# Attention probabilities transposed by VectorE and a trip through DRAM instead of by TensorE

## The chip, the core and the metric

The kernel runs on one core of one Trainium2 chip. The metric is the device time of one execution in microseconds, as the median of several executions. One profiled execution gives the trace; its own time stands beside its span below.

## The reference, cut to what matters

One decoder layer over a prompt of 1024 tokens and 32 sample tokens (8 sequences of 4), all in float32, with a model width of 1024. The input is normed and projected (`h @ w_in`) into thirteen parts. Two branches follow: four mLSTM heads (`mq`, `mk`, `mv` with gates) and sliding-window attention with sinks (`aq`, `ak`, `av`; eight query heads over two key/value heads, window 128). Both are gated, projected by `w_m_out` and `w_a_out`, gated again (`ga`, `gm`), summed and projected by `w_out`; a residual and a final norm end it. The change touches the attention of the prompt:

```
s = jnp.einsum('bnqkgd,bnskd->bnkgqs', qg, k.astype(f32)) * (A_HEAD_DIM ** -0.5)
s = jnp.where(mask[None, :, None, None], s, -jnp.inf)
mx = jnp.maximum(jnp.max(s, axis=-1, keepdims=True), sink)
p = jnp.exp(s - mx)
den = jnp.sum(p, axis=-1, keepdims=True) + jnp.exp(sink - mx)
o = jnp.einsum('bnkgqs,bnskd->bnqkgd', p / den, v.astype(f32))
```

Each block of 128 queries sees its own 128 keys and the 128 before them. In the last product the keys are summed over, so the probabilities are wanted with keys on the partitions, while the softmax makes them with queries on the partitions. This turn is what the change does in another way.

## The kernel before

**The stream.** TensorE works through one long list of projections in a fixed order. A job (`job`, `piece`) is one block of 128 output columns against all tokens, in three pieces of 384, 384 and 288 tokens, with each float32 operand split into a high and a low part (`wh`, `wl`, `h_h`, `h_l`) and three products for each of the eight blocks of the model width. The order is `ak`, `av`, `aq` 0 to 3, then `mq`, `mk`, `mv` of heads 0 and 1, `mq`, `mk` of head 2. Then come pairs of jobs multiplied together with fewer products (`block_products`, results `bx`, `bw`, `by`, `bz`), whose operands `t1` to `t4` are sums of blocks of `h` that the generator `sum_blocks` forms; it starts when job `mq` of head 1 starts. Last come the two output projections and `w_out`.

**Work at the side.** Everything else of TensorE's (attention, mLSTM heads, samples, the gates' ada chunk) is written as generators. The planner `Side` keeps a clock `side.now` that each matmul of the stream advances by its estimated length; `side.tick` after each group of three products lets generators take a step when their time has come and the PSUM bank that they ask for is free. A generator yields the lag until its next step and the banks. Each stream of generators has a limit of live ones and a gap between starts: `"m": (2, 35.0)` for the mLSTM heads, `"a": (5,8.0)` for the attention. So the order of TensorE's instructions is set while the program is written out, and it is kept (`in_order`). The other engines' orders follow from it, with loads that can go earlier moved up by the tile scheduler.

**A unit of attention.** `unit(g, b0)` does two blocks of queries for the pair of heads (g, g+4): 16 units in all. It loads queries, keys and values (`uqv`, `ukv`), 12 us later makes scores (`sc`, eight or fewer matmuls), masks and takes maxima on VectorE (`p`, `mx`, `nmx`), exponentials on ScalarE, the reciprocal of the sum on VectorE, and scales `p` (kv head 0 on VectorE, 1 on ScalarE). Then TensorE transposes `p` into the bank `pt` (`tr` with the identity in `cst`, 8 transposes of 128x128, 6 where `b0` is 0), ScalarE and VectorE copy `pt` back over `p`, and 16 (or 12) matmuls make `oT`. ScalarE copies `oT` to SBUF and the result goes to DRAM (`oD`).

**Loads and stores.** All loads and nearly all stores are issued by SyncE's queue (SP) in order: `dma` at once, `store` with a delay of 4.0 of the planner's clock, so that SP doesn't wait for a result that is not there yet. A load of a tensor first issues its own due stores. GpSimd (POOL) issues the stores that turn a block while they write: VectorE transposes within blocks of 32x32 (`V.transpose`, STREAM_TRANSPOSE), and four DMAs then put the blocks of 32 columns in their places in DRAM in runs of 32 floats. `across` (tensors `mkN`, `mvN`) and `stage_c3` of a head (`yhD`) do that. A head's `load` reads `mkN` and `mvN` back (tiles `hkn`, `hv`) with four other loads, and its next step is planned 9 or 10 us later.

**Buffers.** Most SBUF tiles come from one ring of 43 (`ht`); PSUM has two banks for each of `g`, `a`, `b`, `o`. In the trace nearly every instruction of VectorE, ScalarE and GpSimd has line L219 (the wrapper that records the order), matmuls L258, transposes on TensorE L263, DMAs of SP L246.

Of the kernel before, what the change touches and what calls it, by code (L numbers as in the profile page):

```python
# [23 lines left out]
NT = 4  # L24
# [87 lines left out]
class Side:  # L112
# [4 lines left out]
    def __init__(self, each, limits, quiet):  # L117
        self.each, self.free = each, {}
        self.now, self.last, self.quiet, self.products = 0.0, 0.0, quiet, 0
        self.streams = {n: {"max": m, "gap": g, "wait": [], "live": [], "next": 0.0} for n, (m, g) in limits.items()}  # L120
# [52 lines left out]
def body(tc, a):  # L173
    nc = tc.nc
    with ExitStack() as ctx:
# [55 lines left out]
        def store(out, in_):  # L231
            due.append((side.now + 4.0, out, in_))
# [11 lines left out]

        def issue(out, in_, late=False):
            ins = nc.sync.dma_start(out, in_)  # L246
            ins = getattr(ins, "ins", ins)
# [5 lines left out]
        side = Side(stores, {"m": (2, 35.0), "a": (5,8.0), "x": (2, 0.0), "s": (1, 0.0), "g": (1, 0.0)}, 1.5)  # L253
# [553 lines left out]
        def unit(g, b0):  # L807
# [3 lines left out]
            qv, kv_ = ht([128, 4, 128], "uqv"), ht([128, 4, 128], "ukv")  # L811
            q, kT = qv[:, 0:2].rearrange("p c e -> p (c e)"), kv_[:, 0:3].rearrange("p c e -> p (c e)")
            vn = kv_[:, 3], qv[:, 2], qv[:, 3]
# [51 lines left out]
            for j in range(n0, 4):  # L865
                i, hf = divmod(j, 2)
                for kv in range(2):
                    r = slice(64 * kv, 64 * kv + 64)
                    mm(oT[r, i], vn[i + hf][:, r], pT[kv][:, j], start=(hf == 0 or b0 + i == 0), stop=(hf == 1))
            c0 = b0 * 128  # L870
            o = qv[:, 0:2].rearrange("p c e -> p (c e)")
            S.copy(o, oT.rearrange("p c e -> p (c e)"))
            store(oD[g][:, c0:c0 + 256], o)
# [106 lines left out]
        def head_jobs(h):  # L980
            def keep(n, smp, scale):
                def ev(p, acc, c0, w):
# [8 lines left out]
                    store(mD[h][n == "mk"][:, c0:c0 + m], t[:, :m])  # L991
# [29 lines left out]
        def across(h, n, src, c0):  # L1021
            m = src.shape[1]
            t = ht([128, 512], f"{n}t")[:, :m]
            V.transpose(t, src)
            for b in range(0, 128, 32):
                nc.gpsimd.dma_start(mN[n][h][c0:c0 + m, b:b + 32].rearrange("(t p) e -> p t e", p=32), t[b:b + 32].rearrange("p (t e) -> p t e", e=32))  # L1026

        def head(h):
# [89 lines left out]
            def stage_c3(p):  # L1118
# [7 lines left out]
                for b in range(4):  # L1126
                    nc.gpsimd.dma_start(yhD[h][c0:c0 + m].rearrange("c (q i) (b e) -> b i c q e", i=32, e=32)[b], by_block(y[32 * b:32 * b + 32]))  # L1127
# [274 lines left out]
        class head_in:  # L1402
# [3 lines left out]
            def evac(self, c, th, *src):  # L1406
# [6 lines left out]
                if n == "mv":  # L1413
                    across(h, n, src[0], 512 * th)
                else:
                    if src[0] is not t or n == "mq":
                        S.activation(t, src[0], AF.Copy, scale=scale)
                    store(mD[h][n == "mk"][:, HALF[th]], t)
                    if n == "mk":
                        across(h, n, t, 512 * th)  # L1420
# [9 lines left out]
        class gate:  # L1430
# [277 lines left out]
        def ada_gate():  # L1708
            s9 = cst[:, C_S9:C_S9 + 9]
            for j in range(2):  # L1710
# [16 lines left out]
                dma(gbD[:, cj], gb[0:1])  # L1727
                for t in range(NT):
                    dma(gsD.rearrange("(b t) e -> b t e", t=NT)[:, t, cj], gb[1:9])
# [20 lines left out]

        LOADS = [(len(pairs) - 2, 7), (len(pairs) - 1, 6), (len(pairs) - 1, 7)]
# [388 lines left out]
```

## Time and profile before

| | us |
|---|---|
| median of 3 runs | 859.75 (858.84 to 860.07) |
| the profiled execution | 857.75 |
| its span, first to last instruction | 855.9 |
| TensorE (PE) busy in the span | 822.3 |
| VectorE (DVE) busy | 604.1 |
| ScalarE (ACT) busy | 390.5 |
| GpSimd (POOL) busy | 174.7 |

Busy times are unions of an engine's own instructions. PE's matmuls overlap in its pipeline, so the duration of one is longer than the time it adds; the weight loads (PEld) run beside them. The mean granted clock of TensorE is 0.992. Attention lies between 86 and 275 us of the span, the pairs between about 285 and 655 us. The time of the profiled execution is the span and 1.85 us around it, and lies 2.0 us below the median.

### The profile page before, as it was taken

What the parts mean: (1) busy time and instruction counts of PE and PEld (TensorE: products, weight loads), DVE (VectorE), ACT (ScalarE), POOL (GpSimd) and SP (SyncE); (2) the same over time, 40 slices, a digit from 0 to 9 for tenths busy, and PEclk for the clock granted to TensorE, in tenths of its full rate; (3) what the DMA queues carried; (4) which work ended last, traced back from release to release, by engine and by line L of the source; (5) the groups of instructions that cost most, each with busy time, mean ns of one, the idle gap of its engine ahead of it and who ended that gap; (6) DMA issues with size and microseconds to landing.
All of it is one profiled execution on the core that took longest, in us unless ns stands there. A gap on an engine that the chain in (4) does not pass through costs nothing. (4 is left out here: it accounts for less than half of the span.)

```text
span 855.9 us, 15332 instructions
## 1 busy us (share of the span) xinstructions
PE 822.3 (96%) x5139; PEld 686.6 (80%) x5139; DVE 604.1 (71%) x1596; ACT 390.5 (46%) x963; POOL 174.7 (20%) x236
## 2 busy tenths in 40 slices
PE   6899999999999989999999999999999999999984
PEld 3689988789789778888887777777788999967863
DVE  3787785555687778668666565978766669857987
ACT  4672356545564543555444454434443333233334
POOL 0220000330341434211111000000012032532563
PEclk9999999999999999999999999999999999999998
DMA  9995549459756765664444335553436974273322
GB/s 326 366 356 183 150 137 291 134 125 294 214 153 203 214 170 151 194 198 135 129 115 130 115 111 162 160 150 89 116 99 203 345 254 137 82 247 99 111 99 104
DMA packets 125347, 150.82 MB, mean 176 GB/s; under 512 B 29057, under 2 KB 81409, under 8 KB 125237
## 3 DMA queue, kind: packets, MB, share of 16 engines
q1 hardware_dynamic: 121044, 143.55, 53.5%
q0 software_dynamic: 4224, 6.30, 3.6%
q8 instruction: 40, 0.66, 0.3%
q14 instruction: 39, 0.31, 0.1%
HBM read 109.73 MB, written 41.08 MB: 176 GB/s over the span
## 5 line engine op out<-in xcount | busy, mean ns | idle before, releaser
L1127 POOL DMA_DIRECT2D yhD<-yt x48 | 28.9, 608 | 108.3 <-DVE yt L219 86.3
L258 PE MATMUL g_w_ao<-ya,wh_w_ao 128*128 128x384 f32 (+1 forms) x192 | 45.7, 322 | 0.1
L258 PE MATMUL g_w_mo<-ym_l,wh_w_mo 128*128 128x384 f32 (+1 forms) x192 | 45.7, 323 | 0.0
L219 ACT ACTIVATE p<-p,nmx 128x256 f32<-128x256 f32 (+1 forms) x64 | 31.0, 486 | 28.3 <-DVE nmx L219 28.3
L1026 POOL DMA_DIRECT2D mkN<-mkt x44 | 26.9, 618 | 45.5 <-DVE mkt L219 26.0
L219 DVE CUSTOM_DVE_ANT_0 p<-sc,cst,sink 128x256 f32<-128x256 f32 (+1 forms) x64 | 26.1, 463 | 11.4 <-PE sc L258 11.4
L258 PEld LDWEIGHTS g_w_ao<-ya,wh_w_ao 128*128 128x128 f32 x192 | 33.5, 188 | 0.7 <-DVE ya L219 0.6
L258 PEld LDWEIGHTS g_w_mo<-ym_l,wh_w_mo 128*128 128x128 f32 x192 | 33.5, 188 | 0.0
L258 PE MATMUL g_aq<-h_h,wh_aq 128*128 128x384 f32 (+1 forms) x96 | 32.5, 338 | 0.0
L1026 POOL DMA_DIRECT2D mvN<-mvt x40 | 24.7, 624 | 33.6 <-DVE mvt L219 12.5
L258 PE MATMUL g_aq<-h_l,wh_aq 128*128 128x384 f32 (+1 forms) x96 | 31.0, 323 | 0.0
L258 PE MATMUL g_w_mo<-ym_l,wl_w_mo 128*128 128x384 f32 (+1 forms) x96 | 31.0, 323 | 0.0
L258 PE MATMUL g_aq<-h_h,wl_aq 128*128 128x384 f32 (+1 forms) x96 | 31.0, 323 | 0.0
L258 PE MATMUL g_w_ao<-ya,wl_w_ao 128*128 128x384 f32 (+1 forms) x96 | 30.8, 321 | 0.0
L258 PE MATMUL g_mq<-h_h,wh_mq 128*128 128x384 f32 (+1 forms) x72 | 24.7, 344 | 0.8 <-ACT vs L219 0.8
L258 PE MATMUL g_mk<-h_h,wh_mk 128*128 128x384 f32 (+1 forms) x72 | 24.8, 344 | 0.0
L219 POOL TENSOR_TENSOR ya<-yr,ya 128x384 fp32r<-128x384 f32 (+1 forms) x6 | 7.3, 1222 | 80.7 <-DVE hg L219 67.4
L258 PE MATMUL g_mk<-h_l,wh_mk 128*128 128x384 f32 (+1 forms) x72 | 23.2, 323 | 0.0
L258 PE MATMUL g_mk<-h_h,wl_mk 128*128 128x384 f32 (+1 forms) x72 | 23.2, 323 | 0.0
L258 PE MATMUL g_mq<-h_h,wl_mq 128*128 128x384 f32 (+1 forms) x72 | 23.2, 322 | 0.0
L258 PE MATMUL g_mq<-h_l,wh_mq 128*128 128x384 f32 (+1 forms) x72 | 23.2, 322 | 0.0
L219 POOL COPY qs<-mk 128x32 f32<-128x32 f32 x3 | 1.4, 463 | 103.1 <-ACT mk L219 103.1
(1700 smaller groups left out, 2800.9 us busy)
## 6 DMA issues: line engine op xcount, KB each, us to landing
hb<-hD SPq DMA_DIRECT2D x24, 256.0 KB
x<-xT SPq DMA_DIRECT2D x16, 256.0 KB
early_h<-w_ada SPq DMA_DIRECT2D x8, 512.0 KB
hD<-x SPq DMA_DIRECT2D x16, 256.0 KB
adar_ga<-w_ada SPq DMA_DIRECT2D x16, 256.0 KB
wr_ga<-w SPq DMA_DIRECT2D x16, 256.0 KB
wr_gm<-w SPq DMA_DIRECT2D x16, 256.0 KB
taD<-gt SPq DMA_DIRECT2D x16, 256.0 KB
```

The source lines that it names most:

```text
L219: ins = f(*args, **kw)
L258: in_order(nc.tensor.matmul(out, lhsT, rhs, start=start, stop=stop, skip_group_check=more))
L1026: nc.gpsimd.dma_start(mN[n][h][c0:c0 + m, b:b + 32].rearrange("(t p) e -> p t e", p=32), t[b:b + 32].rearrange("p (t e) -> p t e", e=32))
L1127: nc.gpsimd.dma_start(yhD[h][c0:c0 + m].rearrange("c (q i) (b e) -> b i c q e", i=32, e=32)[b], by_block(y[32 * b:32 * b + 32]))
```

## The change

The probabilities of a unit are no longer transposed by TensorE. VectorE transposes them within 32x32 blocks into the tiles that held queries and keys (`uq`, `uk`), eight DMAs of GpSimd's queue put the blocks in place in a DRAM tensor `pD`, and two loads of SP bring them back as `pT`, at least 18.0 of the planner's clock after the stores are written out; the products follow at least 8.0 after the loads. Values are loaded with `pT` into a tile `uv` of their own, not with the queries.

Around it: eight units may live at once instead of five, with a gap of 6.5 instead of 8.0; only one mLSTM head is live until all 16 units are done (`held`); the planner counts the backlog of SP's and GpSimd's queues (`put`, `landed`); ScalarE itself issues the stores of tiles that it wrote (`oD`, the `mq` and `mk` results, the gates `taD` and `tmD`; 69 in all); other stores wait 6.0 instead of 4.0; the stores of the ada gate go through `store` instead of `dma`.

In numbers of instructions: 4195 matmuls and transposes on TensorE instead of 4315, 148 plain copies on ScalarE instead of 164, 65 transposes on VectorE instead of 33 (and 16 copies of `pt` fewer), DMA issues on SP 667 instead of 716, on ScalarE 69 instead of 0, on POOL 260 instead of 132.

```diff
         def tick(self):
             self.each()
-            for st in self.streams.values():
-                if st["wait"] and len(st["live"]) < st["max"] and self.now >= st["next"]:
+            for name, st in self.streams.items():
+                held = name in self.held and self.held[name]()
+                if st["wait"] and not held and len(st["live"]) < st["max"] and self.now >= st["next"]:
                     self.begin(st)
...
-        def store(out, in_):
-            due.append((side.now + 4.0, out, in_))
+        def store(out, in_, by=None):
+            if by is None:
+                due.append((side.now + 6.0, out, in_))
+            else:
+                by.dma_start(out, in_)
...
+        def put(eng, cost):
+            queue[eng] = max(queue[eng], side.now) + cost
+        def landed(eng, least):
+            return max(least, queue[eng] - side.now + (2.5 if eng == "sync" else 4.0))
+        def scatter(out, in_):
+            nc.gpsimd.dma_start(out, in_)
+            put("gpsimd", 0.65)
...
-        side = Side(stores, {"m": (2, 35.0), "a": (5,8.0), ...
+        side = Side(stores, {"m": (2, 35.0), "a": (8, 6.5), ...
...
-            dma(qv[:, 2:4], vnD[:, b0:b0 + 2])
-            if b0:
-                dma(vn[0], vnD[:, b0 - 1])
             yield 12.0, sc_bank[1]
...
-            yield 7.0, "b"
-            pT = [t.rearrange("p i (j e) -> p (i j) e", e=128) for t in p]
+            yield 3.0, ""
+            flat = lambda t: t.rearrange("p c e -> p (c e)")
+            for kv, t in enumerate((qv, kv_)):
+                V.transpose(flat(t)[:, n0 * 128:], flat(p[kv])[:, n0 * 128:])
+                for k in range(4):
+                    scatter(pD[kv][n0:].rearrange("c (q i) (k e) -> k i c q e", i=32, e=32)[k],
+                                        by_block(flat(t)[32 * k:32 * k + 32])[:, n0:])
+            yield landed("gpsimd", 18.0), ""
+            pT = [ht([128, 4, 128], f"pT{kv}") for kv in range(2)]
+            vn = ht([128, 4, 128], "uv")
             for kv in range(2):
-                pt = pb([128, 4, 128], f"pt{g}_{b0}_{kv}")
-                for j in range(n0, 4):
-                    tr(pt[:, j], p[kv][:, j // 2, j % 2 * 128:j % 2 * 128 + 128], ident)
-                if kv:
-                    V.tensor_copy(pT[kv][:, n0:], pt[:, n0:])
-                else:
-                    S.copy(pT[kv][:, n0:], pt[:, n0:])
-            yield 5.0, "o"
+                dma(pT[kv][:, n0:], pD[kv][n0:].rearrange("c p e -> p c e"))
+            dma(vn[:, n0:3], vnD[:, b0 - 1 + n0:b0 + 2])
+            yield landed("sync", 8.0), "o"
...
-            store(oD[g][:, c0:c0 + 256], o)
+            store(oD[g][:, c0:c0 + 256], o, nc.scalar)
...
-                    store(mD[h][n == "mk"][:, c0:c0 + m], t[:, :m])
+                    store(mD[h][n == "mk"][:, c0:c0 + m], t[:, :m], nc.scalar)
...
-                store((taD, tmD)[c][self.i][:, HALF[th]], t)
+                store((taD, tmD)[c][self.i][:, HALF[th]], t, nc.scalar)
...
-                dma(gbD[:, cj], gb[0:1])
+                store(gbD[:, cj], gb[0:1])
...
+        side.held["m"] = lambda: len(side.streams["m"]["live"]) > 0 and len(units_done) < 16
```

The next rows show TensorE's order before at the transposes of unit (1, 2), in the last piece of job `mk` of head 0. Names are output, then inputs, with the tiles' numbers; `x4` is four rows that read alike.

```order
L258 MATMUL g_mk02_2039<-h_h1_584,wl_mk0_1_1544 128x288
L263 MATMUL pt1_2_0_2056<-cst_82,p0_1820 128x128 x4
L263 MATMUL pt1_2_1_2062<-cst_82,p1_1821 128x128 x4
L258 MATMUL oT1_0_2068<-p0_1707,uqv_1476 64x128
L258 MATMUL oT1_0_2068<-p1_1708,uqv_1476 64x128
```

In the changed program the transposes are gone, and the products of unit (1, 2), which stood in job `mv` of head 0, stand in job `mq` of head 1:

```order
L276 MATMUL g_mq10_2458<-h_h0_386,wh_mq1_0_2171 128x384
L276 MATMUL g_mq10_2458<-h_l0_387,wh_mq1_0_2171 128x384
L276 MATMUL g_mq10_2458<-h_h0_386,wl_mq1_0_2172 128x384
L276 MATMUL oT1_2_2486<-pT0_2243,uv_2245 64x128
L276 MATMUL oT1_2_2486<-pT1_2244,uv_2245 64x128
```

They read `pT`, so TensorE's in-order queue now waits there for a load. POOL's queue at the same units, before only with the stores of the heads' keys (`mkN`), in the changed program:

```order
L221 COPY qs_137<-mk0_1797 128x32
L259 DMA pD1_0_0_1415<-uq_1413 32x12x32 x4
L259 DMA pD1_0_1_1416<-uk_1414 32x12x32 x4
L259 DMA mkN0_149<-mkt_1894 32x12x32 x4
L259 DMA pD1_2_0_1538<-uq_1536 32x16x32 x4
L259 DMA pD1_2_1_1539<-uk_1537 32x16x32 x4
L259 DMA mkN0_149<-mkt_2036 32x12x32 x4
```

Eight stores of a unit now stand between any two groups of four that the heads issue. SP's queue at the reloads of these units, in the changed program (`wr_` are weights of later jobs, `gsD` the stores of the ada gate):

```order
L263 DMA wr_mk2_1_3097<-w1 128x512
L263 DMA pT0_2152<-pD1_0_0_1415 128x3x128
L263 DMA wr_mv2_0_3488<-w1 128x512
L263 DMA pT1_2153<-pD1_0_1_1416 128x3x128
L263 DMA uv_2154<-vnD_115 128x256
L263 DMA uq_2231<-qD2_118 128x256
L263 DMA uk_2232<-kD_114 128x384
L263 DMA gbD_803<-gb0_1943 1x512
L263 DMA gsD_804<-gb0_1943 8x512 x4
L263 DMA pT0_2243<-pD1_2_0_1538 128x4x128
L263 DMA pT1_2244<-pD1_2_1_1539 128x4x128
```

A reload waits in this queue for GpSimd's stores to land, and the loads of weights and of later units stand behind it. On TensorE the first product of head 1 (`S1_0`), which stood in the first piece of job `mk` of head 2, now stands at the start of the pair products `bw` that read `t2`.

More of the change, by code (lines that the diff above doesn't have):

```diff
@@ L243, in dma @@
             issue(out, in_, late)
+        queue = {"sync": 0.0, "gpsimd": 0.0}
+        def put(eng, cost):
[5 more added lines that the diff above has]
+            put("gpsimd", 0.65)
         def issue(out, in_, late=False):
             ins = nc.sync.dma_start(out, in_)
+            put("sync", 0.42)
             ins = getattr(ins, "ins", ins)
@@ L251, in issue @@
             free.append(ins)
-        side = Side(stores, {"m": (2, 35.0), "a": (5,8.0), "x": (2, 0.0), "s": (1, 0.0), "g": (1, 0.0)}, 1.5)
+        side = Side(stores, {"m": (2, 35.0), "a": (8, 6.5), "x": (2, 0.0), "s": (1, 0.0), "g": (1, 0.0)}, 1.5)
         def mm(out, lhsT, rhs, start, stop, share=1, more=False):
@@ L810, in unit @@
             n0 = 1 if b0 == 0 else 0
-            qv, kv_ = ht([128, 4, 128], "uqv"), ht([128, 4, 128], "ukv")
+            qv, kv_ = ht([128, 4, 128], "uq"), ht([128, 4, 128], "uk")
             q, kT = qv[:, 0:2].rearrange("p c e -> p (c e)"), kv_[:, 0:3].rearrange("p c e -> p (c e)")
-            vn = kv_[:, 3], qv[:, 2], qv[:, 3]
+            pD = [dp.tile([4, 128, 128], F32, name=f"pD{g}_{b0}_{kv}") for kv in range(2)]
             dma(q, qD[g][:, b0 * 128:b0 * 128 + 256])
             dma(kT[:, n0 * 128:], kD[:, (b0 - 1 + n0) * 128:(b0 + 2) * 128])
-            dma(qv[:, 2:4], vnD[:, b0:b0 + 2])
-            if b0:
-                dma(vn[0], vnD[:, b0 - 1])
             yield 12.0, sc_bank[1]
@@ L1415, in evac @@
                 else:
+                    by = None
                     if src[0] is not t or n == "mq":
                         S.activation(t, src[0], AF.Copy, scale=scale)
-                    store(mD[h][n == "mk"][:, HALF[th]], t)
+                        by = nc.scalar
+                    store(mD[h][n == "mk"][:, HALF[th]], t, by)
                     if n == "mk":
@@ L1726, in ada_gate @@
                 V.tensor_scalar(gb, gb, 0.25, None, op0=ALU.mult)
-                dma(gbD[:, cj], gb[0:1])
+                store(gbD[:, cj], gb[0:1])
                 for t in range(NT):
-                    dma(gsD.rearrange("(b t) e -> b t e", t=NT)[:, t, cj], gb[1:9])
+                    store(gsD.rearrange("(b t) e -> b t e", t=NT)[:, t, cj], gb[1:9])
                 yield 3.0, "b" if j == 0 else ""
```

9 lines of the change are left out of this document (5 added, 4 removed).

## The prediction

> **What bounds the kernel now.** I read the busy times first, then the same by stage, then what TensorE waits for. The first two lines are the page's busy times; then, for three stretches, their start and end, length, busy time of each engine with instructions, granted clock, DMA share and GB/s.
>
> ```profile
> PE 822.3 (96%) x5139; PEld 686.6 (80%) x5139; DVE 604.1 (71%) x1596; ACT 390.5 (46%) x963; POOL 174.7 (20%) x236
> ...
> 0.00:95.00 95.00, 85.01 (x572) 66.64 (x574) 64.74 (x188) 47.65 (x87) 11.62 (x25) 1.00 0.84 293
> 95.00:285.00 190.00, 187.66 (x1434) 164.54 (x1435) 127.01 (x450) 100.52 (x316) 42.44 (x72) 1.00 0.66 189
> 345.00:660.00 315.00, 314.12 (x1846) 250.51 (x1845) 222.15 (x563) 148.42 (x340) 26.28 (x51) 1.00 0.47 138
> ```
>
> TensorE is the bound: in the attention's stretch it works 187.7 of 190 us, and in the pairs after it 314.1 of 315, at full clock. So work that leaves TensorE between 95 and 285 us brings the end forward by as much, as long as no other engine or transfer then makes it wait; behind 345 us there is no slack that could swallow it. What TensorE waits for between 95 and 345 us (total, times, longest):
>
> ```profile
> PE bx L258 <- DVE f3r_w L219: 2.3, 1, 2.3
> PE pt L263 <- ACT p L219: 1.5, 2, 0.8
> PE bw L258 <- DVE t2l L219: 1.2, 1, 1.2
> PE g_mq L258 <- ACT vs L219: 0.8, 1, 0.8
> ```
>
> No load is among them: heads and units bring their operands through DRAM already, and are planned early enough.
>
> **Step 1, removed: 120 transposes on TensorE.** Groups by form (count, busy us, mean ns), then one unit in order of time:
>
> ```profile
> L263 PE MATMUL pt<-cst,p 128*128 128x128 f32 x120 | 16.3, 275 | 1.5 <-ACT p L219 1.5
> L263 PEld LDWEIGHTS pt<-cst,p 128*128 128x128 f32 x120 | 13.8, 140 | 2.8 <-ACT p L219 2.0 <-issue 0.5
> ...
> 259.59 1.09 PE L263 MATMUL pt<-cst,p 128*128 128x128 f32 x8
> 260.44 0.42 PE L258 MATMUL g_mq<-h_h,wh_mq 128*128 128x384 f32 x1
> 260.70 0.34 PE L258 MATMUL g_mq<-h_l,wh_mq 128*128 128x384 f32 x1
> 260.87 0.34 PE L258 MATMUL g_mq<-h_h,wl_mq 128*128 128x384 f32 x1
> ```
>
> The 275 ns of one is its way through the pipeline, not what it adds. Matmuls of the stream start 0.17 us apart (260.70, 260.87). Without the transposes the one at 260.70 would have started 0.17 after 259.59, so eight cost 260.70 - 259.59 - 0.17 = 0.94 us, 0.117 each; the weight loads' 13.8 us for 120 say 0.115. I take 13.8 us off TensorE. With them goes the wait of `pt` for ScalarE's `p`, 1.5 us in the list above: together 15.3.
>
> **Step 2, added: a way through VectorE, GpSimd, DRAM and SP, and a wait of TensorE at its end.** The rows nearest to its parts are the heads' own transposes and stores, of the same shape and through the same queue (min/median/max ns; us to landing), and the copies that go:
>
> ```profile
> L219 DVE STREAM_TRANSPOSE mkt<-mkv x2: 703/703/703, 329.6 to 337.7; 128x512 f32<-128x512 f32 x2
> L219 DVE COPY p<-pt x16: 539/684/692, 112.3 to 260.7; 128x512 f32<-128x512 f32 x12, 128x384 f32<-128x384 f32 x4
> L219 ACT COPY p<-pt x16: 458/568/595, 112.6 to 261.5; 128x512 f32<-128x512 f32 x12, 128x384 f32<-128x384 f32 x4
> L1127 POOL DMA_DIRECT2D yhD<-yt x48: 582/617/722, 248.1 to 452.4; - x48
> DMA to landing us min/median/max: 2.0/3.5/6.5
> ```
>
> VectorE gets 32 transposes of at most 0.70 (22) and loses 16 copies of 0.68 (11): +11 on 127 of 190 us. ScalarE loses 16 of 0.57 (9). POOL gets 128 issues of 0.617 = 79 us on 42: 121 of about 175 us, 69%. None of the three becomes the bound. A unit takes 1.4 for its two transposes, 8 x 0.62 = 4.9 for the issues and 3.5 to 6.5 for the landing, so 10 to 13 us from the transposes to the data in DRAM; another head's four issues in between add 2.5. The plan gives it 18. Then SP loads `pT` and `uv`, planned at least 8 ahead of `oT`; banks and the gap between units leave about half of them more. What is late there stops TensorE, and the whole stream with it. How late, no row shows. The nearest are the heads' reloads of tensors written the same way, with six loads in a row and 9 to 10 planned ahead: what ScalarE and VectorE waited for them (12 loads of each tensor):
>
> ```profile
> ACT hkn L219 <- DMA hkn<-mkN: 11.6, 7, 4.1
> DVE hv L219 <- DMA hv<-mvN: 10.2, 5, 4.2
> ```
>
> As a bound from above each unit waits (11.6 + 10.2)/12 = 1.8 us, 29 in all; from below none, since TensorE shows no wait for a load. I take 2.5: nearer to nothing, because the heads' waits also never reached TensorE and three loads land sooner than six, but some units have only the least lead of 8.
>
> **The load on the DMA engines** decides about that lead. `pD` is written and read once: 12 units of 512 KB and 4 of 384 KB, 7.9 MB each way, 15.7 in all. On 190 us x 189 GB/s = 35.9 MB this makes 51.6 MB in some 176 us, 293 GB/s. The start of the kernel moves just that, with the engines busy 0.84 of the time. So it fits, with bursts that lie above it.
>
> A rule speaks against GpSimd's stores. The Trainium skill, SBUF — State Buffer, section "A bandwidth-pool intuition that's wrong (but worth ruling out)", has a GpSimd DMA that takes some 620 ns alone take some 3100 ns beside a VectorE copy, since VectorE holds the port through which the descriptors are written. By that, 128 issues would hold POOL for an estimated 397 us on top of its 42, where some 176 are left, and the sum would be about 260 us worse. This trace has the 620 but not the 3100: 722 ns at most, beside a VectorE that is busy two thirds of the time.
>
> **Step 3, ScalarE issues 69 stores, SP 49 DMAs fewer.** SP's row for the store of `oD`, and the longest of what SP waited for between 95 and 345 us:
>
> ```profile
> L246 SPq DMA_DIRECT2D oD<-uqv x16: 319/320/396, 119.9 to 274.8; - x16
> ...
> SPq L246 <- ACT uqv L219: 23.6, 11, 8.6
> SPq L246 <- ACT mk L219: 17.2, 8, 4.6
> SPq L246 <- DVE gb L219: 9.9, 1, 9.9
> ```
>
> At 0.32 an issue costs ScalarE 22 us, at most 12 of them in the attention's stretch (37 stores), where it is busy 100 of 190 and loses 9: between nothing and, if each evacuation came 0.32 late for TensorE, 22. TensorE's only wait for a copy of the stream's results is the 0.8 of `g_mq` behind `vs`, so I take 0. In return the three waits shown leave SP's queue, which helps the loads behind them; as TensorE waits for no load, 0 as well. The longer delay of the other stores (6.0 for 4.0) and the ada gate's stores cost nothing: a reload issues them when it needs them, and the readers come long after. The rest of the planner's changes only move work.
>
> **Step 4, what is late next: `bw` behind `t2l`.** `sum_blocks` starts with job `mq` of head 1, and its loads and splits on VectorE end in the waits of 1.2 (`bw`) and 2.3 (`bx`, behind a head's factors). Units (2, 0) to (3, 6) transposed behind that start: 4 x 6 and 12 x 8 make 120 over four groups, so two groups hold 60, 6.9 us of TensorE. If the chain keeps its length, TensorE arrives 6.9 us earlier and waits that much more; if the holding back of head 1 frees VectorE, the 3.5 us of waits go. Ends -3.5 and +6.9; I take +1.0, nearest to the rows as they are.
>
> **Sum.** -13.8 - 1.5 + 2.5 + 0 + 1.0 = -11.8. The profiled execution took 857.75 (span 855.9 and 1.85 around it), so 845.95; the median lies 2.0 higher at 859.75, so 848.0.
>
> **Rivals.**
> - *Reloads late in every unit (slower).* The heads' late ones were 11.6/7 = 1.7 us late. At 1.7 in each of 16 units TensorE loses 27 instead of 2.5: 848 + 24.5 = 872. It decides from (15.3 - 1.0)/16 = 0.9 us a unit on. For it: a burst of loads on top of 293 GB/s, and the reloads' place in SP's order behind weights that wait for buffers. Against it: the leads in step 2. 11%.
> - *GpSimd's issues stretched (slower).* POOL keeps up as long as 42 + 128 d stays under 175, d under 1.04 us; at 1.2 it runs 21 us behind, and TensorE with it: about 869. The longest row is 0.72, so 2%. This is the rule's mechanism, and the trace does not bear its figure out.
> - *The sum blocks take it back.* Step 4 at +6.9: 854. For it: the wait stands there already. 17%.
> - *The full gain.* No wait at `oT` and the 3.5 us gone: 848 - 2.5 - 4.5 = 841. 15%.
> - *Nothing comes of it*, the added waits equal to what is removed: within 0.2%. 5%.
>
> **How the numbers follow.** My forecast, 843 to 851, has 50%. A difference within 0.2% (1.7 us) is about what a measurement of this kernel can't tell from none. Faster holds the forecast, the sum blocks and the full gain: 82%. The same: 5%. Slower: the two slow rivals, 13%. The range 842 to 860 holds the forecast, the sum blocks, part of the full gain and of no change, and leaves out the two slow rivals and the lower part of the full gain, some 2 in 10. The predicted time is 848.0.
>
> **What would show it.** Step 1: no `pt` rows, PE's busy time down by about 14 us and the stretch from `sc` of unit (0, 0) to `oT` of (3, 6) shorter by as much. Step 2: PE's waits for `oT` by a load of `pT` or `uv`, in total about 2.5; POOL's rows for `pD` at 0.6 us with landings below 7; DMA share between 95 and 270 us at 0.8 or more. Step 3: ScalarE's stores without waits of TensorE for its copies. Step 4: `bw` behind `t2l` with 1 to 4 us. The prediction is wrong if `oT` waits in most units, if POOL is busy nearly throughout that stretch, or if the waits of `bw` grow to 7.

## The result and the profile after

The changed kernel took 884.34 us in the median (881.78 to 887.11) beside 859.3 for the kernel before on the same chip: a ratio of 1.0292, 95% interval 1.025 to 1.0335. It is slower, and the forecast of 848.0 and the range up to 860 missed it. The profiled execution has a span of 880.2 us, 24.3 more than before.

Busy times, the DMA engines in the 40 slices, and for some stretches length, busy time of PE, PEld, DVE, ACT, POOL with instructions, granted clock, DMA share and GB/s, all of the changed kernel (the share adds up the times of all packets, so it can pass 1):

```profile
PE 823.4 (94%) x5019; PEld 683.3 (78%) x5019; DVE 614.7 (70%) x1612; ACT 384.6 (44%) x947; POOL 252.6 (29%) x364
...
DMA  9996669999988776655353444444454875372322
...
95.00:285.00 190.00, 167.85 (x1163) 143.57 (x1160) 117.47 (x417) 84.77 (x275) 113.64 (x184) 0.94 0.91 250
120.00:140.00 20.00, 18.01 (x114) 16.31 (x114) 16.64 (x65) 9.99 (x33) 11.81 (x19) 1.00 0.94 256
140.00:160.00 20.00, 18.47 (x152) 15.64 (x153) 10.54 (x48) 11.40 (x41) 14.65 (x25) 0.91 1.07 336
180.00:200.00 20.00, 17.15 (x114) 14.56 (x112) 9.36 (x31) 8.65 (x30) 16.97 (x28) 0.91 1.03 294
200.00:220.00 20.00, 15.93 (x104) 12.84 (x105) 11.75 (x44) 9.69 (x32) 9.03 (x14) 0.83 0.97 294
220.00:240.00 20.00, 15.60 (x97) 12.59 (x96) 10.68 (x35) 9.73 (x33) 10.48 (x18) 0.91 0.99 287
```

Two things stand out. TensorE has 120 instructions fewer and is busy 1.1 us *longer*, with a granted clock of 0.83 to 0.91 in four of these rows, where it was 1.00 before. And the DMA share, 0.66 in the attention's stretch before, is 0.91 now and about 1 for much of the time between 140 and 240 us. Before, the same stretch had TensorE busy for 187.7 of its 190 us; now for 167.9. What TensorE waits for in the whole execution, the longest rows whose kind was not there before (total, times, longest; `bx` waited for VectorE's `f3r_w` before, 2.3):

```profile
PE oT L276 <- DMA uv<-vnD: 10.7, 4, 3.5
...
PE sc L276 <- DVE mx L221: 5.0, 3, 2.5
...
PE bx L276 <- DVE mvt L221: 2.5, 1, 2.5
PE bx L276 <- DVE zt L221: 2.5, 1, 2.5
PE g_mv L276 <- ACT mk L221: 2.4, 1, 2.4
PE gp L276 <- ACT adas_ga L221: 2.3, 1, 2.3
PE g_mq L276 <- ACT mk L221: 1.6, 1, 1.6
```

The reloads are late at `oT` (`uv` is the last of a unit's three loads), but only in four units; the others are waits for VectorE and ScalarE. One of those at the scores shows how a late load of a head gets there, in order of time (start, duration, instruction, in brackets what its engine waited for before it):

```profile
198.07 0.06 DVE L221 MEMSET hv<- 128x3 f32 x1 [7.06 <-DMA hv<-mvN]
202.39 0.48 PE L276 MATMUL sc<-uk,uq 64*128 64x128 f32 x2 [2.48 <-DVE mx L221]
```

VectorE had waited 7.06 us for the load `hv`, then more for two others, and came late to the maxima `mx` for which the scores wait. Not each row has such a cause: `bx` waits 2.5 for `zt` without any traffic too (e1 below). ScalarE's copy of `oT` waited for TensorE in ten units (before in eight, 10.5 us), and what comes after it in ScalarE's order waited too:

```profile
ACT pT L221 <- PE oT L276: 27.2, 10, 6.3
```

Why the engine is busy longer is seen in one stop, in order of time (start, duration, instructions):

```profile
191.96 0.34 PE L276 MATMUL g_mq<-h_h,wl_mq 128*128 128x384 f32 x1
195.06 1.09 PE L276 MATMUL oT<-pT,uv 128*64 128x128 f32 x16 [2.76 <-DMA uv<-vnD]
...
196.83 0.52 PE L276 MATMUL g_mq<-h_h,wh_mq 128*128 128x384 f32 x1
197.15 0.52 PE L276 MATMUL g_mq<-h_l,wh_mq 128*128 128x384 f32 x1
197.47 0.52 PE L276 MATMUL g_mq<-h_h,wl_mq 128*128 128x384 f32 x1
```

TensorE stops for 2.76 us. Soon after it goes on, the same matmuls start 0.32 us apart instead of 0.17. The windows around it, and one after the next two stops, show the granted clock (the third figure from the end): full in the first and the last row, exactly a half in the two between:

```profile
192.30:195.06 2.76, 0.00 (x1) 0.00 (x0) 0.00 (x0) 0.00 (x0) 2.28 (x4) 1.00 1.08 340
196.57:199.97 3.40, 3.34 (x11) 2.83 (x9) 0.60 (x2) 1.00 (x4) 2.11 (x4) 0.50 0.95 172
203.40:210.21 6.81, 5.45 (x31) 4.43 (x30) 3.90 (x17) 3.81 (x13) 4.45 (x7) 0.50 0.90 256
210.23:229.00 18.77, 18.77 (x140) 15.14 (x139) 6.36 (x22) 7.25 (x25) 10.09 (x17) 1.00 0.98 307
```

SP had issued the load of this `uv` at 188.50, 6.6 us before the products could start. So such a stop can be paid twice: its own length, and then 3.4 or 6.8 us at half speed. In all TensorE is without work for 56.8 us (span less busy time) and works 823.4; the first experiment says what they would be without the traffic.

### The profile page after: what moved, and what is told of

Same layout as the page of the kernel before. It is cut to its first block, busy times and chain, and to the rows that moved or that the text cites. A ratio compares the mean times of both kernels' runs of the same rounds, so it can differ in the third digit from the quotient of the medians.

```text
span 880.2 us, 15326 instructions
## 1 busy us (share of the span) xinstructions
PE 823.4 (94%) x5019; PEld 683.3 (78%) x5019; DVE 614.7 (70%) x1612; ACT 384.6 (44%) x947; POOL 252.6 (29%) x364
## 3 DMA queue, kind: packets, MB, share of 16 engines
q0 software_dynamic: 8320, 14.17, 7.0%
## 5 line engine op out<-in xcount | busy, mean ns | idle before, releaser
L259 POOL DMA_DIRECT2D pD<-uq x64 | 41.0, 647 | 65.6 <-DVE uq L221 60.7
L259 POOL DMA_DIRECT2D pD<-uk x64 | 40.8, 644 | 2.5 <-DVE mxs L221 0.7
L276 PE MATMUL g_w_ao<-ya,wl_w_ao 128*128 128x384 f32 (+1 forms) x96 | 30.8, 321 | 0.0
L276 PE MATMUL oT<-pT,uv 128*64 128x128 f32 x240 | 19.6, 312 | 10.7 <-DMA uv<-vnD 10.7
L259 POOL DMA_DIRECT2D mvN<-mvt x40 | 24.7, 624 | 16.4 <-DVE f3r_w L221 11.5
L276 PEld LDWEIGHTS oT<-pT,uv 128*64 128x64 f32 x240 | 15.2, 155 | 15.6 <-issue 9.3
```

What stands on the lines that cost most here:

```text
L259: nc.gpsimd.dma_start(out, in_)
L276: in_order(nc.tensor.matmul(out, lhsT, rhs, start=start, stop=stop, skip_group_check=more))
```

## The experiments

The theories: **A**, the traffic through DRAM fills the DMA engines and what is loaded comes late (A1: the cost lies in the waits at `oT`; A2: all loads of that stretch are late). **B**, the other order of the work (held head, eight units). **C**, ScalarE's stores hold TensorE up. Two came later: **R**, not the bytes but the order on SP, the number of transfers under way or tiles held too long; **T**, of these the tiles alone, which the ring then hands out late. Ratios are to the kernel before on the same chip, with 95% intervals.

### Which part costs

**e1, nothing through DRAM.**

```diff
-                for k in range(4):
-                    scatter(pD[kv][n0:]..., by_block(flat(t)[32 * k:32 * k + 32])[:, n0:])
-            pT = [ht([128, 4, 128], f"pT{kv}") for kv in range(2)]
+            pT = [t.rearrange("p i (j e) -> p (i j) e", e=128) for t in p]
-            for kv in range(2):
-                dma(pT[kv][:, n0:], pD[kv][n0:].rearrange("c p e -> p c e"))
```

> The changed kernel without the way through DRAM: the 128 stores into pD and the 32 reloads are left out, and the products of oT read p where it lies (so the turning is left out too; VectorE still transposes). All else stays: eight units, the held head, uv loaded late, ScalarE's stores. Theory A (the way through DRAM costs: its traffic fills the DMA engines between 120 and 270 us and the reloads come late): 841 to 849 us, TensorE's waits for oT under 3 us, granted clock 1.00 in the stretch. Theory B (the other order of the work costs: eight units, the held head, stores on ScalarE): 870 us or more, much like the changed kernel's 884.

845.57 us, 0.9835 (0.981 to 0.986). Its busy times and attention stretch:

```profile
PE 807.8 (96%) x5019; PEld 671.8 (80%) x5019; DVE 611.0 (73%) x1612; ACT 384.4 (46%) x947; POOL 172.1 (20%) x236
...
95.00:285.00 190.00, 188.85 (x1407) 163.54 (x1404) 147.49 (x509) 104.13 (x326) 47.40 (x82) 1.00 0.72 215
```

Theory A, as expected, and B is out as the whole story; traffic and the waits for it go together here, and e2 and e10 tell them apart. With the same 5019 instructions TensorE works 807.8 us here and 823.4 in the changed kernel: 15.6 us are lost to the lower clock. Idle are 841.1 - 807.8 = 33.3 here and 56.8 there: 23.5 more. Together 39.1, the whole difference of the spans (880.2 - 841.1).

**e2, all the traffic, nobody waits for the reloads.** Products read `p` as in e1, `uv` is loaded with `uq`; stores and reloads stay.

```diff
-            pT = [ht([128, 4, 128], f"pT{kv}") for kv in range(2)]
+            pT = [t.rearrange("p i (j e) -> p (i j) e", e=128) for t in p]
+            back = [ht([128, 4, 128], f"pT{kv}") for kv in range(2)]
...
-                dma(pT[kv][:, n0:], pD[kv][n0:].rearrange("c p e -> p c e"))
+                dma(back[kv][:, n0:], pD[kv][n0:].rearrange("c p e -> p c e"))
```

> The changed kernel with all of its traffic, but nobody waits for the reloads: the 128 stores into pD and the 32 reloads run as they are, the products of oT read p where it lies (turning left out), and uv is loaded with uq and uk at the start of the unit. Theory A1 (what costs is that TensorE stops at oT for late reloads, and what follows from those stops): 845 to 855 us. Theory A2 (the traffic itself costs everywhere: the heads' loads, the weights and the other loads come late too): 865 to 880 us, with the waits moved to other loads. Theory B (the other order of the work): 875 us or more.

890.72 us, 1.037 (1.034 to 1.0401): slower still, and above the range of A2 too. A1 falls as the whole cause. What TensorE waits for most between 95 and 300 us, then some of VectorE's waits there:

```profile
PE sc L276 <- DVE mx L221: 21.2, 5, 6.3
...
DVE hv L221 <- DMA hv<-mvN: 7.9, 2, 6.3
DVE et L221 <- DMA et<-nmd: 6.0, 3, 2.7
...
DVE p L221 <- DMA pT<-pD: 5.0, 3, 3.5
...
DVE p L221 <- DMA qD<-aqr: 3.4, 1, 3.4
```

No wait at `oT` is left, and 21.2 us stand at the scores instead. VectorE, in order, waits for the heads' loads and for the tile that it wants to write `p` into, whose last user, a load or a store, is not done. So the lateness is not bound to waiting for the reloads. (e2 also holds the tile of `uv` longer, which may be part of the 6 us that it lies above the changed kernel.)

**e3, ScalarE's 69 stores back on SP.**

```diff
-            store(oD[g][:, c0:c0 + 256], o, nc.scalar)
+            store(oD[g][:, c0:c0 + 256], o)
...
-                        by = nc.scalar
+                        by = None
```

> The changed kernel with ScalarE's 69 stores put back on SP (6.0 late, as the others). Theory C (ScalarE's issues hold up TensorE: its waits for mk, adas_ga and mx behind ScalarE add up to 14 us): 865 to 872 us, and those waits go. Theory A (the reloads): 882 to 892 us, since SP then has 69 more issues ahead of the reloads, and the waits at oT stay or grow.

890.55 us, 1.0364 (1.0336 to 1.0392). C is wrong: the stores on ScalarE save some 6 us in the changed kernel.

**e7, the stores alone in the kernel before.**

```diff
-            store(oD[g][:, c0:c0 + 256], o)
+            store(oD[g][:, c0:c0 + 256], o, nc.scalar)
...
-                dma(gbD[:, cj], gb[0:1])
+                store(gbD[:, cj], gb[0:1])
```

> The kernel before with only the stores changed: ScalarE issues the stores of its own results, the others go 6.0 late, and the ada gate's rows are stores too; p is turned by TensorE as before. The prediction's step 3 says nothing changes: 857 to 861 us. If the stores' waits in SP's queue hold loads that matter (as the 6 us between the changed kernel and the same with its stores on SP suggest): 852 to 856 us.

859.55 us, 1.0003 (0.9985 to 1.002): nothing, as the prediction had it. The stores matter only where SP's queue is late.

**e10, every DMA in its place, a quarter of the bytes.** The one that decides between bytes and everything else.

```diff
-                    scatter(pD[kv][n0:]..., by_block(...)[:, n0:])
+                    scatter(pD[kv][3:]..., by_block(...)[:, 3:])
...
-                dma(pT[kv][:, n0:], pD[kv][n0:].rearrange("c p e -> p c e"))
+                dma(pT[kv][:, 3:], pD[kv][3:].rearrange("c p e -> p c e"))
```

> The changed kernel with every DMA of the way through DRAM in its place, and a quarter of its bytes: only the last of p's four 128x128 blocks is stored into pD and reloaded, and all products of oT read that one (so three quarters of the turning are left out). The 128 issues on GpSimd, the 32 reloads on SP, the tiles, the waits and the plan are as they are. Theory A2 (the bytes fill the engines): 846 to 856 us, no waits for uv, hardly any half clock. Theory R (the order on SP, the eight transfers that may be under way, or tiles that are held too long): 870 to 884 us.

853.64 us, 0.991 (0.9889 to 0.9931).

```profile
95.00:285.00 190.00, 187.15 (x1384) 161.37 (x1386) 142.33 (x499) 101.16 (x318) 111.81 (x202) 1.00 0.80 228
...
PE sc L276 <- DVE mx L221: 2.5, 4, 1.3
PE bx L276 <- DVE mvt L221: 2.0, 1, 2.0
```

Same issues, same waits, same tiles, and the stretch is back at full clock with a DMA share of 0.80. The bytes, with the packets that carry them, are the cost, 32.8 us of it by the ratios; what R names is left, by itself, with the 6.5 us that e10 lies above e1. The bytes that went are 5.76 MB on GpSimd's queue (14.17 less 8.41) and as many on SP's, there in 11264 packets fewer.

That full engines are what links bytes and late loads is argued, not shown. The mean share of a stretch is no criterion: e2 and e11 (below) have 0.83 in the same stretch and lose more than the changed kernel, while the half (e4) has 0.82 and loses nothing that can be told. GpSimd's stores of `mkN`, the same in all, land after 3.4 us in the median in e1, 4.4 in the changed kernel, but 4.1 in e10.

**e6, 3.67 MB of other loads left out.**

```diff
-                    raws.append(ht([128, 512], f"adar_ga{j}{k}"))
-                    dma(raws[-1], a["w_ada"][4 + j, :, k])
+                    if k == 0:
+                        raws.append(ht([128, 512], f"adar_ga{j}{k}"))
+                        dma(raws[-1], a["w_ada"][4 + j, :, k])
+                    else:
+                        raws.append(raws[0])
```

> The changed kernel with 14 of the ada gate's 16 weight loads left out (its products all read the first one, so the gate is not the reference's); the way through DRAM is whole. 3.67 MB go from 120 to 250 us. By the first hardware queue's cost on the engines (143.55 MB in 53.5% of 16 engines over 855.9 us, 19.6 bytes a ns each) that is 11.7 us of all 16 engines. Theory A2 (the engines are full there, whoever's bytes they are): 862 to 874 us, with fewer stops of TensorE and less time at half clock. If instead the way through DRAM is late by its own latency, whatever else moves: 880 to 886 us.

878.57 us, 1.0232 (1.0211 to 1.0252): between the two expectations, 5.2 us off the changed kernel by the ratios. The share in the stretch is 0.87 (234 GB/s) for 0.91. These bring 5.2/3.67 = 1.4 us a MB, the 11.5 MB that e10 takes off 32.8/11.5 = 2.9. By the intervals the 5.2 can be 1 to 9, so whether bytes of other loads weigh less is likely but not sure, and why stays open.

**e8, more lead; e11, no tiles of its own for the reloads.**

```diff
-            yield landed("gpsimd", 18.0), ""
+            yield landed("gpsimd", 24.0), ""
...
-            yield landed("sync", 8.0), "o"
+            yield landed("sync", 16.0), "o"
```

> The changed kernel with the reloads and the products of oT planned later: at least 24 instead of 18 from the transposes to the reloads, and 16 instead of 8 from the reloads to oT. If the stops come from a plan that is too tight by some us: 855 to 868 us, and the waits for uv go. Theory A2 (full engines): 876 to 890 us, since the same bytes fill the same stretch; the waits for uv shrink, but tiles are held longer, and the waits move to other loads and to tiles that come free late.

895.24 us, 1.0424 (1.0389 to 1.046), above both ranges. TensorE's matmuls wait for no `uv` by the profile any more, and other waits of 2.5 to 5.8 us have come, for example:

```profile
PE oT L276 <- issue: 5.8, 1, 5.8
PE g_mk L276 <- ACT mk L221: 4.5, 3, 3.2
PE gp L276 <- ACT adas_ga L221: 4.0, 1, 4.0
...
313.02 0.49 SPq L263 DMA_DIRECT2D uv<-vnD  x1
```

The longest is still one at `oT`, for which the profile shows no releaser. SP issued the last unit's second `pT` and `uv` only at 312.59 and 313.02, behind two loads of `wr_gm`, and the products started at 317.46: a late reload again, as far as can be seen. A longer lead in the plan did not help there, since SP issued late.

```diff
-            pT = [ht([128, 4, 128], f"pT{kv}") for kv in range(2)]
-            vn = ht([128, 4, 128], "uv")
+            pT = [t.rearrange("p i (j e) -> p (i j) e", e=128) for t in p]
+            vn = kv_
```

> The changed kernel with the whole way through DRAM, but no tiles of its own for the reloads: pT goes back into p's tiles and vn into that of uk, which are idle by then. 48 of the tiles that the ring of 43 hands out fall away. Theory T (the ring hands out tiles late, since those of a unit are held some 26 us longer): 855 to 872 us. Theory A2 (bytes): 878 to 888 us, much like the changed kernel.

902.81 us, 1.0482 (1.0445 to 1.0518), above both ranges. This doesn't settle T. The load of `vn` must now wait until GpSimd's stores have read the tile, and TensorE waited 29.2 us in five units for it; the edit made a new wait of its own.

### How much of it pays, and the plan

**e4, e9, e13: half, a quarter, two fifths** of the way; the rest of `p` is turned by TensorE as before. The edit of e9; e13 has the condition `if b0`, e4 turns kv 0 of every unit in the new way. Where e9, e12 and e13 send nothing away, a unit yields 2.0, at least 3.0 and 5.0 instead of 18.0 and 8.0.

```diff
+            away = (0,) if b0 in (0, 4) else ()
-            for kv, t in enumerate((qv, kv_)):
+            for kv in away:
...
+                for kv in range(2):
+                    if kv in away:
+                        continue
+                    pt = pb([128, 4, 128], f"pt{g}_{b0}_{kv}")
+                    for j in range(n0, 4):
+                        tr(pt[:, j], ...)
```

> The changed kernel with half of the way through DRAM: p of the first pair of heads (kv 0) goes through pD, p of the second is turned by TensorE and copied by VectorE as in the kernel before (60 transposes stay, 7.9 MB go). If what is lost comes from full DMA engines (theory A), the loss falls by more than half, since the share of DMA between 120 and 270 us falls from 0.94 to about 0.8: 850 to 858 us, faster than before or the same. If each late reload costs by itself whatever the load: the middle of an undisturbed 848 and 884, 866 us. Theory B: 875 us or more.

858.66 us, 1.0 (0.9979 to 1.002): most of the loss is gone, as theory A has it.

> The changed kernel with a quarter of the way through DRAM: only p of kv 0 in every second unit (b0 0 and 4) goes through pD; the rest is turned by TensorE as before (about 90 of 120 transposes stay). 16 of the 66 us that the whole way takes of all 16 engines, where the kernel without it leaves about 53 free between 95 and 285 us. Theory A2 with a threshold (no loss while the engines have room): 853 to 857 us, the gain of 30 transposes (3.4 us) and what ScalarE's stores bring. If the loss is in proportion to the bytes: 858 to 861 us.

852.33 us, 0.993 (0.9911 to 0.9949).

> The changed kernel with p of kv 0 of twelve of the sixteen units (all but b0 0) through DRAM: 48 of 120 transposes go, 26 of the 66 us of all 16 engines come. Theory A2 with a threshold: 849 to 853 us, at or below the quarter's 852.3. If the loss grows with the bytes from the start: 854 to 858 us, between the quarter and the half (858.7).

858.09 us, 0.9977 (0.9958 to 0.9996): the second expectation, not the threshold.

**e12, the plan alone:** `away = ()`, all 120 transposes on TensorE, everything else of the change in place.

> The changed kernel with nothing through DRAM: all 120 transposes on TensorE and the copies as before; the rest of the change stays (eight units, the held head, ScalarE's stores, uv loaded late). Were the quarter's gain of 6.8 us that of its 28 transposes (3.2 us) and of the plan, the plan alone brings 3 to 4 us: 854 to 857 us. If the plan is worth nothing by itself: 858 to 861 us.

865.79 us, 1.0074 (1.0046 to 1.0102). Not expected by either: this plan costs. TensorE waits for a head's state there, late by 4.0 and 2.8 us:

```profile
PE S L276 <- DVE C L221: 6.8, 2, 4.0
```

With the ratios times 859.1, the changed plan gives this row, though a unit's lags differ as said: 0 transposes less 865.5; 28: 853.1; 48: 857.1; 60: 859.1; 120: 884.2, and 844.9 for 120 less with no traffic. A straight line between the first and the last would be 860.7, 857.3, 855.2 and 844.9. Above that line lie -7.6, -0.2, +3.9 and +39.3: up to two fifths the way through DRAM costs nothing that can be told from the scatter of the plan (e15 to e19 show how wide that is), and the second half costs nine tenths of it.

**e14, the whole change without the held head.**

```diff
-        side.held["m"] = lambda: len(side.streams["m"]["live"]) > 0 and len(units_done) < 16
```

> The changed kernel without the hold on head 1: heads start 35 apart as before, the way through DRAM is whole, eight units at once. If the hold is what costs in the plan: 875 to 880 us. If the bytes decide (theory A2), earlier heads put their own DRAM traffic on top of the units': 884 to 895 us.

881.81 us, 1.0278 (1.0252 to 1.0303), between the two expectations and not told from the changed kernel. The loss doesn't hang on the hold.

**e15, e16, e17, e18, e19: the quarter and the plan taken apart.** e15 is the kernel before with the quarter and six units; e16 is e9 with `"a": (5, 8.0)`; e17 is e12 with `"a": (5, 8.0)` and no held head; e18 is the quarter on e17 with `"a": (6, 8.0)`; e19 is e17 with `away = (0,) if b0 == 4 else ()`.

> The kernel before with nothing but the quarter: p of kv 0 in the units with b0 0 and 4 goes through DRAM by VectorE, GpSimd and SP; six units at once instead of five (with five the tiles' ring closes on itself); stores, loads of v and heads as before. If the plan's edits only cost, this gains what 28 transposes are worth and no more is lost: 852 to 856 us. If the quarter's gain needs the plan: 857 to 861 us.

859.83 us, 1.0014 (0.9998 to 1.003): no gain that can be told from none.

> The quarter in the changed kernel's plan with five units at 8.0 instead of eight at 6.5, head 1 held. If eight units at once cost by themselves: 848 to 851 us. If they are what hides the way through DRAM: 855 to 862 us. Neither: 852, as the quarter with eight.

860.28 us, 1.0024 (1.0005 to 1.0044). In two other plans the quarter does not bring what it brought in e9.

> Nothing through DRAM, five units at 8.0, no head held; of the change stay ScalarE's stores and uv loaded after the transposes' place instead of with uq and uk. ScalarE's stores alone measured the same as before. If uv loaded late costs the 6 to 7 us of the plan: 863 to 867 us. If the hold and the eight units cost them: 857 to 861 us.

851.05 us, 0.9914 (0.9894 to 0.9933), faster than both kernels without any way through DRAM; of the variants that leave nothing out only the quarter (e9, 0.993) comes as near. Its edits against the kernel before are ScalarE's stores with the later other stores (nothing by e7), `uv` in a tile of its own, loaded shortly before it is used, `oT` copied into a tile of `p`, and transposes that are planned slightly later. Which of the last three brings it was not told apart. Between 95 and 660 us no wait of TensorE is longer than 1.1 us, and after the attention it works without a gap:

```profile
PE bw L276 <- ACT bw L221: 1.1, 1, 1.1
...
285.00:345.00 60.00, 60.00 (x381) 49.65 (x380) 45.86 (x138) 31.03 (x83) 23.38 (x38) 1.00 0.68 189
```

Before, this stretch had 3.5 us of waits (`bx`, `bw`) and a clock of 0.97. The 13.7 us between e12 and e17 (1.0074 less 0.9914) are what the held head and the eight units cost when nothing goes through DRAM.

> e17 with the quarter (p of kv 0 in the units with b0 0 and 4 through DRAM) and six units at 8.0 instead of five. If the transposes' time comes on top of e17's gain: 847 to 850 us. If the added tiles and issues use it up: 851 to 858 us.

868.02 us, 1.0095 (1.0061 to 1.013), above both ranges. A new wait of 5.7 us (`bx` for ScalarE's `mk`) and one of 3.0 stand in it.

> e17 with an eighth of the way: p of kv 0 in the four units with b0 4 goes through DRAM, five units at 8.0. 16 transposes go, 1.8 us of TensorE: 848.5 to 850 us if that comes on top of e17; 851 to 856 us if the added tiles and issues use it up.

854.46 us, 0.9947 (0.9929 to 0.9966). On e17's plan the way through DRAM brings nothing. The quarter gained in one plan of four (e9, against e15, e16 and e18), so its gain looks like luck of the plan and can't be put down to its 28 transposes.

## Why the prediction was wrong, step by step

By the ratios on 859.1: the plan +6.4 (e12), the transposes and their copies away -20.6 (e12 to e1, which also have other lags in a unit), the way's DMAs and waits with a quarter of the bytes +6.5 (e1 to e10), the other bytes +32.8 (e10 to the change). Sum +25.1. The forecast had -15.3, +2.5 and +1.0.

**Step 1 was right.** PE's busy time falls from 822.3 to 807.8 in e1: 14.5 for the 13.8 forecast (up to 1.7 of it from 3.4 us at half clock at 302 us, which only the kernel before has), and the wait of `pt` goes with them. Without the traffic's cost the change would stand at e1's 844.9, between the forecast and the rival of the full gain (841).

**Step 2's load on the DMA engines is the step that failed.** It took 293 GB/s as room for the stretch because the kernel's start moves that at a share of 0.84. But the row of the stretch itself, quoted there, has 189 GB/s at 0.66, which is 286 at a full share: below the 293 needed. "So it fits" was wrong by the very rows shown. The term that it let stand at 2.5, the reloads' lateness, was mis-sized by this. The queues of the kernel before and then of the changed one (packets, MB, share of 16 engines over the span) say what the way costs:

```profile
q1 hardware_dynamic: 121044, 143.55, 53.5%
q0 software_dynamic: 4224, 6.30, 3.6%
```

```profile
q1 hardware_dynamic: 125252, 136.99, 51.2%
q0 software_dynamic: 8320, 14.17, 7.0%
q10 hardware_dynamic: 9936, 14.42, 4.8%
```

GpSimd's queue: 7.0% of 880.2 less 3.6% of 855.9 is 30.8 us of all 16 engines for 7.87 MB. SP's and ScalarE's together: 56.0% of 880.2 less 53.5% of 855.9 is 35.0 us for 7.86 MB net, 14144 packets more. The way takes 65.8 us where the forecast's 349 GB/s made it 45, and where the stretch had 190 x (1 - 0.66) = 64.6 free, or 53 in e1's order (share 0.72). It was about full without any burst. The runs showed, in place of "2.5 at `oT`", 39.3 for the whole way (e1 to the change), 32.8 of it with the bytes (e10 to the change) and 10.7 in the waits at `oT`.

**Its other terms held.** VectorE +10.6 (forecast 11), POOL 252.6 - 174.7 = 77.9 (79). GpSimd's issues, and their landing:

```profile
L259 POOL DMA_DIRECT2D pD<-uq x64: 617/651/782, 103.5 to 267.7; - x64
L259 POOL DMA_DIRECT2D pD<-uk x64: 617/651/713, 106.1 to 270.3; - x64
...
DMA to landing us min/median/max: 2.1/4.6/7.1
```

The longest took 0.78 us. In the kernel before it was 0.78 as well (a row of `mkN`; the prediction's 0.72 is the most of `yhD`). The landings, 4.6 us in the median and 7.1 at most, lie about where the forecast had them (3.5 to 6.5). The rule of the Trainium skill, SBUF — State Buffer, section "A bandwidth-pool intuition that's wrong (but worth ruling out)", has some 3.1 us for such a DMA beside a VectorE copy; no issue here shows it. That is no test of it: only 12 of the 260 issues run beside a plain copy of VectorE, and these copies last 0.41 us at most.

**Step 3**: nothing by itself (e7), 6 us in the changed kernel (e3). "As TensorE waits for no load, 0 as well" held only as long as the loads were on time.

**"The rest of the planner's changes only move work"** is the second step that failed. Held head and eight units cost 13.7 us without the way (e12 against e17), and `uv` loaded late, with the small edits beside it, gains 7.6 (e7 against e17, 1.0003 less 0.9914). What moves work moves some stop of 2 to 5 us in or out.

**Step 4** came in size at `bw` (1.1 and 0.5), but not in its cause: it stands behind ScalarE instead of `t2l`. In e1, without the traffic, `bw` is not in the list and `bx` waits 1.2 and 2.5; the sum blocks did not take the gain back.

**The slow rival** named the place and the direction (reloads late, a burst on top of the base load), at 11%. Its measure, 1.7 us a unit at `oT` and a threshold of 0.9, would not have caught it: the trace shows 10.7/16 = 0.7 a unit. The loss came to 25 us all the same, since late loads of the heads also stopped VectorE and so TensorE elsewhere, and since most stops are followed by half clock: 15.6 of the 39.1 us, a term that the prediction did not have at all.

**Left open.** SP waited 29.7 us in ten times for ScalarE's stores of `oD` in the changed kernel, 10.1 in four in e1:

```profile
SPq L263 <- DMA oD<-pT: 29.7, 10, 6.1
```

A late `oT` makes its store late, and SP waits for that store before it issues its next DMA. How much of the 32.8 us is this loop and how much the engines' own fullness was not told apart; e17, which loses nothing, has 17.2 in eight of the same wait. Nor were the reload's many small packets told apart from their bytes.

## What to carry to other kernels

Ask of a way through DRAM first what share of the DMA engines the stretch has left, and convert bytes into share with that stretch's own GB/s and share, or with the queue's time for packets of the same size, never with those of a stretch that moves other packets. Price a stop of TensorE at its length plus what the clock can lose after it. The cost of such a way need not be in proportion: here half of it lost nothing that could be told and the whole lost 39 us. Try the plan without the change as well: edits to a planner's limits are worth a run of their own, since here they moved the time by 14 us, as much as all the transposes are worth.

## What the runs showed of the hardware that was not expected

A short stop can halve TensorE's clock. After the 2.76 us stop shown, matmuls ran at 0.32 us instead of 0.17 for 3.4 us, which is 1.6 us of loss. Seven stretches of 3.4 us and one of 6.8 between 140 and 590 us make 30.7 us at half clock, at most 15 lost: nearly the whole of the 15.6. The Trainium skill, TensorE: Matmul & The Clock Gate, section "What's actually happening", has a window of 3413 ns and half the clock after an idle one: the length agrees with the 3.4 and 6.8 us here, but less than a whole window of idleness was enough. Not every stop does it: after 2.36 us before `g_mv` at 252.3 (the changed kernel) and after 2.5 us at 544.9 (e1) the clock stayed full:

```profile
252.40:256.00 3.60, 3.60 (x30) 3.18 (x31) 3.25 (x16) 1.51 (x3) 1.36 (x3) 1.00 0.42 117
...
545.00:549.00 4.00, 4.00 (x18) 3.25 (x19) 3.94 (x7) 1.26 (x2) 0.00 (x0) 1.00 0.17 66
```

The traces show what decides. In each run all stretches at half clock begin on one grid of 3.413 us. For all 20 traces of this case, between 75 and 640 us, TensorE's idle time by the profile was added up for each step of a run's grid that ran at full clock. Where it was 1.9 us or more, the next step was at half clock in 54 of 54 cases; from 1.5 to 1.9 in 7 of 20; from 1.0 to 1.5 in none of 40. Of these steps of the changed kernel, the first holds most of the 2.76 us stop, and the two others share that of 2.36:

```profile
193.15:196.56 3.41, 1.50 (x19) 1.33 (x20) 0.00 (x0) 0.35 (x1) 2.90 (x6) 1.00 1.07 313
247.77:251.18 3.41, 2.18 (x15) 1.86 (x13) 2.48 (x11) 3.41 (x17) 0.00 (x0) 1.00 0.83 246
251.18:254.60 3.42, 2.29 (x23) 1.87 (x23) 3.17 (x15) 2.22 (x5) 0.00 (x0) 1.00 0.70 199
```

TensorE is idle for 1.91 us of the first, and for 1.23 and 1.13 of the others. So where a stop of 2 to 3 us falls on the grid decides whether it is paid twice, and that is luck.

The way's packets move fewer bytes a ns than the kernel's others. GpSimd's stores of `pD` take 30.8 us of all 16 engines for 7.87 MB, 16 bytes a ns on each engine. The reloads come in packets of 512 bytes: the trace has 36736 of that size in the changed kernel and 21376 in e1, and the 15360 more take 28.4 us of 16 engines, 0.03 us each, 17 bytes a ns. The first queue of the kernel before makes 143.55 MB / 7326 us = 19.6. So some 59 of the 65.8 us are the way's own packets; in the rest other packets took longer.
